# Splitting the output projection of all eight output blocks into two halves of the contraction

## The chip, the cores and the metric

The kernel runs on one core of one Trainium2 chip. The metric is the device time of one execution in microseconds (us). Before the change it is 1344.11 us, the median of three runs (1343.78 to 1345.62).

## The reference

The reference is one step of a hybrid decoder trunk with two layers, in fp32, on 512 prompt tokens and 8 sequences of 4 tokens (544 columns in all), with a model width of 1024. Cut to what matters here, each layer computes

```
h    = RMSNorm(x) * (1 + scale1) + shift1
proj = h @ w_in                          # q, k, v | u | xr, yg
o    = concat(RMSNorm(attention), RMSNorm(state-space mixer), RMSNorm(recurrent mixer)) @ w_o
x    = x + gate1 * o
h2   = RMSNorm(x) * (1 + scale2) + shift2
x    = x + gate2 * (gelu(conv(h2 @ w_up)) * conv(...)) @ w_down
```

The contraction of `@ w_o` runs over 1024 mixer features: 512 of the attention, 256 of the state-space mixer (S5), 256 of the recurrent one (RG-LRU).

## The kernel before

Everything is kept transposed: features lie on the 128 partitions and tokens on the free axis. The 544 columns are cut into two halves, half 0 with 256 columns and half 1 with 288 (the last 32 are the short sequences). Every product of the large matrices is split for accuracy into three fp32r matmuls (`mm3`, L428): a high part of the weight with a high and a low part of the activation, and a low part of the weight with the high one.

The class `Weights` streams the weights in the order of `weights_order` (L1657). There are six slots (`NW`), each with a high and a low tile; a load is a DMA on SP's queue into one of three staging tiles, a cast on ScalarE to the high part (L416) and a subtraction on VectorE for the low part (L417). A slot is given back by `done`, which at once starts the next load. So the order of the list WO (L43) and the moment of each `done` set when a later weight can be used.

`proj` (L1590 and after) is the output projection. It has eight units i (blocks of 128 output features) and two halves, and the contraction runs over eight chunks k in the order KO = 6, 7, 4, 5, 0, 1, 2, 3: first the recurrent mixer (6, 7), then the state-space mixer (4, 5), last the attention (0 to 3). The chunks 6, 7, 4, 5 are called the first part here, the chunks 0 to 3 the second part. Before the change:

- Three pieces (units 0 to 2, half 0) run their first part and stay open in three PSUM banks (L1617 to L1620).
- Units 0 to 3 run the first part of their other pieces, five pieces in all. `some` (L1606) makes one piece: it waits until its chunks have been emitted, takes a bank, runs the matmuls, and `end` adds gate times the result into x (`residual`, L940) and frees the bank.
- The three open pieces get their second part and end.
- Then come the remaining pieces in a skewed order: (3,0), (4,0), (0,1), (5,0), (1,1), (6,0), (2,1), (7,0), (3,1), then the emission of the normalisation of half 0 for the feed-forward part (`norm_all(0)`), then (4,1), (5,1), (6,1), (7,1). Units 0 to 3 run only their second part here, units 4 to 7 all eight chunks.

After each piece of `some` one `tick` emits the next step of the mixers, with one unit of the attention (its scores, its transposes, its product with v). The last piece of every unit also accumulates the squares of x for the next normalisation (`sq_accum`). The normalisation of half 1 is emitted inside the first group of the feed-forward part (`group`, L911), which runs three units of half 0 first.

The written order is a priority and not the issue order: a list scheduler at compile time places each instruction where its engine is free in its own model, earlier lines first. `urgent` moves the residual and the squares 50 places ahead. On the chip each engine then works in its fixed order. PSUM has eight banks here: `wide` (two pairs) and four single ones, called mb0s in layer 0 and mb1s in layer 1 (fb0, fb1 in the feed-forward part). A bank is chosen when a piece is emitted, the least recently used free one.

Of the kernel before, what the change touches and what calls it, by code (L numbers as in the profile page):

```python
# [39 lines left out]
SKEW = 4  # L40
LAG = 3
KO = (6, 7, 4, 5, 0, 1, 2, 3)
WO = ((4, 8, range(4)), (0, 4, range(4)), (0, 8, range(4, 8)))  # L43
NATT = 1
PIN = True
S12 = (2, 12, 5, 14)
# [210 lines left out]
class Banks:  # L257
# [40 lines left out]
    def one(self, w=512, wide=False, only=None):  # L298

        for z in (only, ()):  # L300
            e = [e for e in self.free if (any(y in e[0] for y in z) if z else not self.apart or self.wide(e[0]) == wide)]
            if e:
                break
        n, b = min(e, key=lambda e: self.used[e[0]])
        self.free.remove((n, b))
        self.touch(n)
        return self.tile[n][:, b, :w]
# [10 lines left out]
def trunk(ctx: ExitStack, tc: tile.TileContext, A, O):  # L318
# [46 lines left out]
    def urgent():  # L365
        return tc.high_priority(HPR)
# [61 lines left out]
    def mm3(out, w, k, r, sl, first, last):  # L428
        a, b = sl
        for i, (wi, ri) in enumerate(((0, 0), (0, 1), (1, 0))):  # L430
            T_.matmul(out, w[wi][:, k, :], r[ri][:, a:b], start=first and i == 0, stop=last and i == 2)  # L431
# [431 lines left out]
    def sq_accum(c, hf):  # L863
        a, b = HALF[hf]
        if c == 0:
            SQ[hf] = sp.tile([128, 288], F32, tag=f"sqacc{hf}", name="sqacc", bufs=1)[:, :b - a]
            act(SQ[hf], x[:, c, a:b], AF.Square)
        else:
            s = W(b - a)
            act(s, x[:, c, a:b], AF.Square)  # L870
            V.tensor_add(SQ[hf], SQ[hf], s)
# [34 lines left out]
    def norm_all(hf, al, sh):  # L906
        yield from norm_stats(hf)
        for _ in norm_half(hf, al, sh, True):
            pass

    def run(g):  # L911
        for _ in g:
            pass
# [26 lines left out]
    def residual(ps, g, c, hf):  # L940
        a, b = HALF[hf]
        stt(x[:, c, a:a + 256], ps[:, :256], g[:, c, 0:1], x[:, c, a:a + 256], OP.mult, OP.add)
        if hf:
            t = sp.tile([128, 32], F32, tag="rs", name="rs")
            tv = t.rearrange("p (b t) -> p b t", t=4)
            V.tensor_tensor(tv, ps[:, 256:288].rearrange("p (b t) -> p b t", t=4),
                            g[:, c, 1:9, None].to_broadcast([128, 8, 4]), op=OP.mult)
            V.tensor_add(x[:, c, NP:NT], x[:, c, NP:NT], t)
# [520 lines left out]
    def background(n=1, lanes=(bg, bga)):  # L1469
        for _ in range(n):  # L1470
            for lane in lanes:
                while lane:
                    try:
                        next(lane[0])
                        break
                    except StopIteration:
                        lane.pop(0)

    def flush():
        while bg or bga:  # L1480
            background()
# [18 lines left out]
    def mixers(l, M):  # L1500
# [66 lines left out]
        for n, i in enumerate(WIN_ORDER[l][GRP:]):  # L1567
# [6 lines left out]
            if n == 11 - GRP:  # L1574
                M.win_done = True
                PS.apart = not UNAP
            start(i, p)
        proj(l, M, tick)

    def proj(l, M, tick):  # L1580
        d = LY[l]
        while d["ada"] < 2:
            background()
        g1 = d["mod"][:, 16:24]
        sh2 = d["mod"][:, 24:32]
        def need(k, hf):
            for _ in range(200):
                if (k, hf) in M.o:
                    return
                tick(NTK)  # L1590
            raise RuntimeError(("never ready", k, hf, M.left))

        def part(o, i, hf, k, first, last):
            a = 0 if i > 3 or k < 4 else 4
            mm3(o, W_[("wo", l, a, i)], k - a, hs[k], HALF[hf], first, last)

        def end(i, hf, o, last=True):
            with urgent():
                residual(o, g1, i, hf)
                PS.put(o)  # L1600
                if last:
                    sq_accum(i, hf)
            if hf:
                W_.done(("wo", l, 0 if last else 4, i))

        def some(i, hf, ks, last=True):  # L1606
            for k in ks:
                need(k, hf)
            o = one(HALF[hf][1] - HALF[hf][0], True, PLAST[0] if (i, hf) in PLAST[1] else ())
            for k in ks:  # L1610
                part(o, i, hf, k, k == ks[0], k == ks[-1])
            end(i, hf, o, last)
            tick()

        o = [one(256, True) for i in range(GRP)]
        for k in KO[:4]:
            need(k, 0)  # L1617
            for i in range(GRP):
                part(o[i], i, 0, k, k == KO[0], False)
        for i in range(4):  # L1620
            for hf in range(2):
                if (i, hf) not in ((0, 0), (1, 0), (2, 0)):
                    some(i, hf, KO[:4], False)
        for k in KO[4:]:
            need(k, 0)
            for i in range(GRP):
                part(o[i], i, 0, k, False, k == KO[-1])
        for i in range(GRP):
            end(i, 0, o[i])
        for i, hf in skewed(GRP):  # L1630
            some(i, hf, KO if i > 3 else KO[4:])
            if (i, hf) == (7 - SKEW, 1):
                flush()
                run(norm_all(0, d["al2"], sh2))
        late.append(norm_all(1, d["al2"], sh2))
        assert not M.CH.c
        PS.apart = False

    def skewed(skip=0):
        seq = []  # L1640
        for i in range(8 + SKEW):
            if skip <= i < 8:
                seq.append((i, 0))
            if i >= SKEW:
                seq.append((i - SKEW, 1))
        return seq
# [11 lines left out]
    def weights_order():  # L1658
        for l in range(L):
            for i in WIN_ORDER[l]:  # L1660
                yield ("win", l, i), A["win"][l, i], 8
            for a, b, u in WO:
                for i in u:
# [218 lines left out]
```

## Time and profile before

| | |
|---|---|
| median of three runs | 1344.11 us |
| time of the profiled execution | 1342.55 us |
| span, first to last instruction | 1340.8 us |
| TensorE matmul busy | 1275.7 us (95%) |
| VectorE busy | 871.8 us (65%) |
| ScalarE busy | 599.7 us (45%) |
| mean granted TensorE clock | 0.982 of full |

Busy time of TensorE is the union of modelled matmul durations, so a stretch at half the clock also counts as busy; the column of the granted clock has to be read beside it. PE is TensorE, DVE is VectorE, ACT is ScalarE, SP is the queue that issues most DMAs. Times in the rows are counted from the start of the span. In the output projections nearly all matmuls have the one line L431, in the helper `mm3`; the output tile (mb0s, mb1s, wide) and the width (256 or 288) tell the pieces apart.

### The profile page before, as it was taken

The page shows a single profiled execution, that of the slowest core. Times are in us where ns is not written, and L with a number is a line of the kernel's source. Part 1 is how long each engine was busy: PE and PEld are TensorE (multiplying, and loading weights), DVE is VectorE, ACT ScalarE, POOL GpSimd, SP SyncE. Part 2 cuts the span into 40 slices and gives each one's busy share as a digit, 9 for nine tenths or more (in the row PEclk, how much of TensorE's full clock was granted, in tenths as well). Part 3 has the DMA queues.
Part 4 walks back from the last instruction along what each step waited for, and adds up shares of the span by engine and source line. Part 5 has one row for each costly group of instructions (what it writes and reads, how often), then busy time and mean ns, then how long its engine had stood idle before and what let it go on. Part 6 is the DMA issues. An engine that isn't in the chain of part 4 may idle for free.

```text
span 1340.8 us, 26252 instructions
## 1 busy us (share of the span) xinstructions
PE 1275.7 (95%) x10406; PEld 1173.5 (88%) x10406; DVE 871.8 (65%) x2521; ACT 599.7 (45%) x1196; POOL 48.7 (4%) x82
## 2 busy tenths in 40 slices
PE   5889988989999999999999999899999999999998
PEld 2666776989989998999999887579999999999998
DVE  7877786987564454545548796668865455645651
ACT  4558756465341333233335558655634234323430
POOL 0121010000110000000000001000000000000000
PEclk8999988999999999999999999898999999999999
DMA  9776660436553454335524533112322322233221
GB/s 355 238 239 212 190 188 15 171 124 208 191 199 112 156 189 160 125 125 189 177 73 139 148 94 87 45 54 79 111 89 70 107 84 85 88 95 95 80 77 51
DMA packets 71099, 178.23 MB, mean 133 GB/s; under 512 B 15376, under 2 KB 22448, under 8 KB 70976
## 3 DMA queue, kind: packets, MB, share of 16 engines
q1 hardware_dynamic: 64096, 162.08, 37.7%
q0 software_dynamic: 4960, 11.68, 2.7%
q10 hardware_dynamic: 1920, 2.79, 0.8%
q8 instruction: 82, 1.34, 0.4%
q14 instruction: 41, 0.34, 0.1%
HBM read 159.37 MB, written 14.34 MB: 130 GB/s over the span
## 4 chain that ended last, share of the span: by engine, by line
PE 63%; DVE 4%; ACT 3%; DMA 2%; issue 1%; POOL 0%; SPq 0%; DVEq 0%; POOLq 0%; ACTq 0%
PE wide L431 33%; PE fb1w L431 9%; PE fb0w L431 7%; PE fb1s L431 4%; PE mb1s L431 3%; PE fb0s L431 3%; PE fb0s L577 2%; DMA araw<-in_wada_dram 1%; ACT pm L378 1%; PE mb1s L1282 1%; DVE f L381 1%; DMA f<-kscr 0%; ACT whi L416 0%; ACT L378 0%; PE mb1s L1121 0%
## 5 line engine op out<-in xcount | busy, mean ns | idle before, releaser
L431 PE MATMUL wide<-hh,whi 128*128 128x256 f32 (+1 forms) x1368 | 402.0, 295 | 5.0 <-ACT hh L937 2.0
L431 PE MATMUL wide<-hl,whi 128*128 128x256 f32 (+1 forms) x1368 | 399.6, 292 | 0.0
L431 PE MATMUL wide<-hh,wlo 128*128 128x256 f32 (+1 forms) x1368 | 396.9, 290 | 0.0
L417 DVE TENSOR_TENSOR wlo<-raw,whi 128x1024 fp32r<-128x1024 f32 (+2 forms) x184 | 212.1, 1153 | 195.8 <-ACT whi L416 191.9
L416 ACT CAST whi<-raw 128x1024 fp32r<-128x1024 f32 (+2 forms) x184 | 182.4, 991 | 317.6 <-PE wide L431 171.9
L431 PEld LDWEIGHTS wide<-hh,whi 128*128 128x128 f32 x1368 | 258.9, 190 | 21.1 <-issue 11.2
L431 PEld LDWEIGHTS wide<-hh,wlo 128*128 128x128 f32 x1368 | 261.2, 191 | 2.5 <-issue 2.3
L431 PEld LDWEIGHTS wide<-hl,whi 128*128 128x128 f32 x1368 | 259.7, 190 | 4.0 <-issue 3.6
L431 PE MATMUL wide<-mid,whi 128*128 128x256 f32 (+1 forms) x582 | 111.3, 288 | 0.0
L381 DVE SCALAR_TENSOR_TENSOR f<-wide,prm,f 128x511 f32<-128x511 f32 x236 | 100.0, 484 | 0.0
L431 PEld LDWEIGHTS wide<-mid,whi 128*128 128x128 f32 x582 | 91.4, 188 | 0.4 <-issue 0.4
L937 ACT CAST mid<-f 128x544 fp32r<-128x544 f32 x44 | 28.5, 647 | 127.5 <-DVE f L1718 124.2
L431 PE MATMUL wide<-mid,wlo 128*128 128x256 f32 (+1 forms) x291 | 83.8, 288 | 0.0
L378 ACT ACTIVATE f<-f 128x544 f32<-128x544 f32 x50 | 33.0, 659 | 87.4 <-DVE f L1708 82.5
L431 PE MATMUL fb1w<-hh,whi 128*128 128x256 f32 (+1 forms) x240 | 69.3, 289 | 2.0 <-ACT hh L903 1.5
L431 PE MATMUL fb1w<-hl,whi 128*128 128x256 f32 (+1 forms) x240 | 69.5, 290 | 0.0
L431 PE MATMUL fb1w<-hh,wlo 128*128 128x256 f32 (+1 forms) x240 | 68.9, 287 | 0.0
L431 PE MATMUL fb0w<-hh,whi 128*128 128x256 f32 (+1 forms) x224 | 66.0, 295 | 2.4 <-ACT hh L903 2.4
L381 DVE SCALAR_TENSOR_TENSOR x<-wide,mod,x 128x256 f32<-128x256 f32 x53 | 25.6, 483 | 63.4 <-PE wide L431 63.3
L431 PE MATMUL fb0w<-hl,whi 128*128 128x256 f32 (+1 forms) x224 | 65.0, 290 | 0.0
L431 PE MATMUL fb0w<-hh,wlo 128*128 128x256 f32 (+1 forms) x224 | 64.7, 289 | 0.0
L378 ACT ACTIVATE pm<-pm,st 128x256 f32<-128x256 f32 (+3 forms) x128 | 57.4, 476 | 11.3 <-DVE st L1284 9.2
(612 smaller groups left out, 2558.2 us busy)
## 6 DMA issues: line engine op xcount, KB each, us to landing
raw<-in_wup_dram SPq DMA_DIRECT2D x88, 512.0 KB, 3.6
araw<-in_wada_dram SPq DMA_DIRECT2D x28, 1024.0 KB, 5.2
raw<-in_wada_dram SPq DMA_DIRECT2D x29, 512.0 KB, 5.3
raw<-in_wdn_dram SPq DMA_DIRECT2D x32, 448.0 KB, 3.4
raw<-in_win_dram SPq DMA_DIRECT2D x24, 512.0 KB, 4.5
raw<-in_wdn_dram SPq DMA_DIRECT2D x16, 512.0 KB, 3.6
raw<-in_wo_dram SPq DMA_DIRECT2D x16, 256.0 KB, 4.0
raw<-in_wo_dram SPq DMA_DIRECT2D x8, 512.0 KB, 3.7
```

The lines of the kernel that those rows point to most:

```text
L378: return S.activation(out, in_, f, bias=bias, scale=scale, **kw)
L381: return V.scalar_tensor_tensor(out, a, s, b, op0=op0, op1=op1, **kw)
L416: S.copy(hi, raw)
L417: V.tensor_sub(lo, raw, f32(hi))
L431: T_.matmul(out, w[wi][:, k, :], r[ri][:, a:b], start=first and i == 0, stop=last and i == 2)
L577: T_.matmul(ps[32 * g:32 * g + 32], silu[:, k + i, :], raw[:, i, g], start=k + i == 0, stop=k + i == 7, skip_group_check=True)
L937: S.copy(dst[0], src)
L1282: T_.matmul(pv, M.q[c][:, j * 128:j * 128 + 128], M.kz[:, :, k0:k0 + nk], start=True, stop=True)
```

## The change

The number of split units becomes a constant, WOS = 8. All eight units run their first part ahead of the second: three open pieces as before, then thirteen pieces of the first part in place of five, then the second part of all sixteen. The weights come as sixteen half loads for each layer (first parts of units 0 to 7, then second parts) in place of eight half and four whole ones.

```diff
-WO = ((4, 8, range(4)), (0, 4, range(4)), (0, 8, range(4, 8)))
+WOS = 8
+WO = ((4, 8, range(WOS)), (0, 4, range(WOS)), (0, 8, range(WOS, 8)))
...
         def part(o, i, hf, k, first, last):
-            a = 0 if i > 3 or k < 4 else 4
+            a = 0 if i >= WOS or k < 4 else 4
...
-        for i in range(4):
+        for i in range(WOS):
             for hf in range(2):
                 if (i, hf) not in ((0, 0), (1, 0), (2, 0)):
                     some(i, hf, KO[:4], False)
...
         for i, hf in skewed(GRP):
-            some(i, hf, KO if i > 3 else KO[4:])
+            some(i, hf, KO if i >= WOS else KO[4:])
             if (i, hf) == (7 - SKEW, 1):
                 flush()
                 run(norm_all(0, d["al2"], sh2))
```

## Rows read from the trace of the kernel before

**Rows 1.** Windows, layer 1: length, PE, PEld, DVE, ACT, POOL busy, clock, DMA, GB/s.
```profile
858.20:887.20 29.00, 27.75 (x188) 21.61 (x188) 18.76 (x68) 16.84 (x55) 0.00 (x0) 0.88 0.23 68
887.20:904.08 16.88, 16.88 (x139) 15.56 (x138) 10.44 (x34) 9.45 (x27) 0.00 (x0) 1.00 0.10 32
904.08:907.41 3.33, 0.71 (x5) 0.27 (x3) 3.19 (x14) 0.90 (x3) 0.00 (x0) 0.96 0.00 0
907.41:914.04 6.63, 6.47 (x25) 6.12 (x26) 4.87 (x14) 2.66 (x5) 0.00 (x0) 0.51 0.00 0
...
921.13:936.18 15.05, 15.05 (x114) 14.79 (x113) 14.15 (x42) 9.09 (x16) 0.00 (x0) 1.00 0.35 106
936.18:947.33 11.15, 9.59 (x80) 9.11 (x78) 9.91 (x34) 4.14 (x9) 0.00 (x0) 1.00 0.46 141
```
**Rows 2.** Waits of PE from 840 to 960: us in total, times, longest.
```profile
PE mb1s L431 <- ACT hh L937: 2.1, 2, 1.1
...
PE wide L479 <- DVE qr L381: 1.6, 1, 1.6
PE fb1w L431 <- ACT hh L903: 1.5, 1, 1.5
```
**Rows 3.** ScalarE's timeline in layer 1: start, us; the weight casts of units 6, 7.
```profile
911.46 1.05 ACT L416 CAST whi<-raw 128x1024 fp32r<-128x1024 f32 x1 [2.76 <-PE mb1s L431]
...
914.10 1.05 ACT L416 CAST whi<-raw 128x1024 fp32r<-128x1024 f32 x1 [0.99 <-PE wide L431]
```
**Rows 4.** Windows, layer 0, the same columns as of layer 1.
```profile
226.20:259.60 33.40, 33.34 (x258) 33.13 (x259) 31.31 (x113) 12.42 (x21) 0.00 (x0) 0.95 0.38 127
259.60:274.56 14.96, 14.96 (x115) 14.78 (x113) 14.88 (x44) 7.38 (x12) 1.67 (x3) 1.00 0.59 194
274.56:288.93 14.37, 10.68 (x97) 9.46 (x95) 13.08 (x43) 6.08 (x14) 0.54 (x1) 1.00 0.45 131
288.93:298.00 9.07, 9.07 (x56) 8.97 (x57) 5.95 (x25) 6.60 (x15) 0.00 (x0) 0.81 0.14 56
```
**Rows 5.** Chain that ended last, 921 to 960: start, us: a half-1 piece, four chunks.
```profile
921.29 1.60 PE mb1s L431 x12
```
**Rows 6.** The chain in layer 1, 840 to 960: a half-0 piece of eight chunks.
```profile
918.49 2.81 PE wide L431 x24
```
**Rows 7.** VectorE's timeline: first low parts of the next activations, layers 0 and 1.
```profile
273.07 1.67 DVE L381 SCALAR_TENSOR_TENSOR hl<-half,mod,hh 128x256 fp32r<-128x256 f32 x4
...
929.79 1.27 DVE L381 SCALAR_TENSOR_TENSOR hl<-half,mod,hh 128x256 fp32r<-128x256 f32 x3
```
**Rows 8.** VectorE by line and form, 921.13 to 947.33: busy us, mean ns.
```profile
L417 DVE TENSOR_TENSOR wlo<-raw,whi 128x1024 fp32r<-128x1024 f32 x5 | 6.1, 1218 | 0.0
L381 DVE SCALAR_TENSOR_TENSOR half<-x,al,sqacc 128x256 f32<-128x256 f32 x8 | 3.4, 477 | 0.0
...
L871 DVE TENSOR_TENSOR sqacc<-sqacc,half 128x288 f32<-128x288 f32 x6 | 2.7, 452 | 0.2
L381 DVE SCALAR_TENSOR_TENSOR x<-mb1s,mod,x 128x256 f32<-128x256 f32 x5 | 2.4, 476 | 0.1
...
L948 DVE TENSOR_TENSOR x<-x,rs 128x32 f32<-128x32 f32 x5 | 0.9, 182 | 0.0
L946 DVE TENSOR_TENSOR rs<-mb1s,mod 128x32 f32<-128x32 f32 x5 | 0.9, 179 | 0.0
```
**Rows 9.** VectorE by line and form, 259.60 to 288.93: two of five table groups.
```profile
L612 DVE TENSOR_TENSOR f<-pw,f 128x384 f32<-128x384 f32 x2 | 1.1, 554 | 0.0
...
L616 DVE TENSOR_TENSOR f<-pw,f 128x384 f32<-128x384 f32 x1 | 0.5, 548 | 0.0
```
**Rows 10.** Line L417 over the span: ns min/median/max, forms.
```profile
L417 DVE TENSOR_TENSOR wlo<-raw,whi x184: 678/1224/1228, 21.2 to 1301.6; 128x1024 fp32r<-128x1024 f32 x136, 128x896 fp32r<-128x896 f32 x32, 128x512 fp32r<-128x512 f32 x16
```
**Rows 11.** DMA issues of the page: count, KB each, us to landing.
```profile
raw<-in_wo_dram SPq DMA_DIRECT2D x16, 256.0 KB, 4.0
raw<-in_wo_dram SPq DMA_DIRECT2D x8, 512.0 KB, 3.7
```

## The prediction

> **What bounds the kernel now.** I read the page first: in the table, PE's busy time of 95% of the span says that time can only come from PE's few gaps, from stretches at the lower clock, or from other work that delays PE. The 40 slices of the page put the gaps into the mixers and just behind them, so I cut the two output projections into windows and read the waits, the chain and the engines' timelines there.
>
> Layer 1 is where the change has something to win. PE works on at full clock until 904.08, and then in 3.33 us it is busy for only 0.71; the next 6.63 us run at a granted clock of 0.51, which is the 1.2 GHz level [rows 1]. The waits name the end of the attention's normalisation, 1.6 us for its scale and 2.1 us in all for the casts of its output [rows 2]. Why PE had nothing else is in ScalarE's timeline: the weights of units 6 and 7 are cast at 911.46 and 914.10 only, since a slot comes free when (0,1) and (1,1) are done, and these wait for the attention of half 1 [rows 3].
>
> Layer 0 has no such hole: from 226.20 to 274.56 PE is busy 33.34 of 33.40 and 14.96 of 14.96 us [rows 4]. What a split could fill there is nothing.
>
> Behind both projections stands a second limit. The last piece of half 0, (7,0), ends at about 259.6 and 921.1. From there the normalisation of half 0, the last residuals and squares, and the weights of the next matrix all pass VectorE; the first half-1 matmul of the feed-forward part comes at 288.93 and 947.33. VectorE is busy 14.88 + 13.08 of 29.33 us in the one layer and 14.15 + 9.91 of 26.20 us in the other [rows 1, 4].
>
> **Part 1: what the stall gives back.** In layer 1 the idle time is 3.33 - 0.71 = 2.6 us, and the low clock costs 6.63 x (1 - 0.51) = 3.2 us, together 5.8 us [rows 1]. A half-1 piece of four chunks takes 1.60 us [rows 5]; a half-0 piece of eight takes 2.81, so one of four 1.41 [rows 6]. The change frees the first parts of units 4 to 7 from the attention: 4 x (1.41 + 1.60) = 12.0 us, less any part that ran early anyway. After 887.2 there are then 12.0 us of first parts, 8 x 1.41 = 11.3 us of half-0 second parts and some attention for the 20.2 us up to 907.41. PE no longer runs dry; I take the whole 5.8 us. Nothing hides what is late next: the half-0 pieces behind it. The bounds are 0 (the added pieces wait on banks) and 5.8 plus 1.25, the idle part of the window from 858.20 [rows 1]. In layer 0 the value is 0, bounds 0 and 0.1 [rows 4].
>
> **Part 2: what moves ahead of the normalisation.** Before, the four pieces (4,1) to (7,1) run all eight chunks behind (7,0). After, their first parts, 4 x 1.60 = 6.4 us [rows 5], run ahead of it. PE's total is the same, so (7,0) ends 6.4 us later in each layer, less what part 1 gives: layer 0 at 259.6 + 6.4 = 266.0, layer 1 at 921.1 - 5.8 + 6.4 = 921.7. The cover behind (7,0) shrinks from 15 us [rows 1, 4] to 8.6. The first low part of the new activations is complete 9.1 us behind (7,0) in layer 1 (929.79 plus one third of 1.27) and 13.9 us in layer 0 (273.07 plus a quarter of 1.67) [rows 7]. So PE also idles at the start of the feed-forward part, by 0.5 to 5 us. That idle is no term of its own as long as half 1 comes later still.
>
> **Part 3: the stretch from (7,0) to half 1.** Its VectorE work is not reduced: five low parts of weights at 1.218 us, sixteen instructions of 0.477 of the half-0 normalisation, six residuals, seven sums of squares, two scale calculations [rows 8]. In layer 1 it took 26.20 us with VectorE 24.06 busy; behind 921.7 it ends at 947.9, which is 0.6 us later than now. The bounds are -1.5 (only the busy 24.06) and +2.5 (idle as now, and two residual groups of 0.84 more queued behind). In layer 0 it took 29.33 us, of which nine instructions on tables for the next layer at about 0.55 us make 4.9 us (in five groups of rows, of which the first and the last stand in [rows 9]). They are not needed here. The bounds from 266.0 are 23.1 us (busy time without tables, +0.2) and 29.3 us (all of it again, +6.4). I take 26.2 us, the row of layer 1, which has the same work without tables: 292.2, so +3.3.
>
> **Part 4: the added instructions.** Per layer there are eight more residuals: four of half 0 at 0.476 and four of half 1 at 0.476 + 0.182 + 0.179 = 0.84 us, 5.3 us [rows 8]. Eight half-size low parts at 0.68 in place of four whole ones at 1.22 add 0.6 us [rows 10]. All 5.9 us fall on VectorE ahead of (7,0). In layer 1 it is busy 18.76 + 10.44 of 45.9 us there, which hides them [rows 1]. In layer 0 it is busy 31.31 of 33.40 us [rows 4], but tables and other early work fill its holes, and the stretch grows by 6.4 us. I take 0; if the cover fails, 5.9 - 2.1 = 3.8 us at most in layer 0, and no reason gives a gain. Queued behind an urgent residual on VectorE are the attention's masks, and for these PE's transposes; each can be late by 0.5 us, which costs nothing while PE has pieces. Per layer there are four more load triggers on SP, and the half loads land in 4.0 us against 3.7 [rows 11]; three staging tiles and 3 us of PE for a unit hide that. Eight more ticks per layer find the attention already emitted: 0.
>
> **Part 5: the clock.** PE's idle time ahead of half 1 grows in layer 1 from 1.5 us [rows 2] to some 5: its pieces end near 930.4, three units of half 0 fill 8.4. After the comparable gap in layer 0 the stretch from 288.93 ran at 0.81 and took 9.07 us [rows 4]. Layer 1 fell to no low clock there; I take 0.4 us, from 0 to 9.07 x 0.19 = 1.7.
>
> The Trainium skill has a rule that speaks against the change, in "TensorE: Matmul & The Clock Gate", section "A second HAM failure mode: psum-queue depth-cycling": a kernel that cycles its groups through the banks lets PE idle briefly between groups, and the clock swings. Here the pieces on rotating banks from 921.13 to 936.18 show PE busy 15.05 of 15.05 us at clock 1.00 [rows 1], so no term comes of it; by the rule the last rival below gains weight.
>
> **The sum.** Layer 0 +3.3, layer 1 +0.6 + 0.4: +4.3 us. On the profiled execution of 1342.55 us (span 1340.8 and 1.75 around it) that is 1346.9; this execution lies 1.56 us under the median of 1344.11, so the median is forecast at 1348.4 us.
>
> **The rivals.** All times are on the median.
>
> *Rival 1, not slower: half 1 follows PE and not VectorE.* If the scheduler puts the weights of the fourth to sixth feed-forward unit (3 x 1.22 us) behind the normalisations, half 1 comes 11.15 us after PE's pieces, as now, and 947.33 becomes 941.5; layer 0 keeps its time. 1344.1 - 5.8 = 1338.3. It decides where VectorE's work behind (7,0) falls to 8.6 + 11.15 = 19.8 us; 24.06 less 3.7 is 20.4, just short. For it: PE's stall in layer 1 is real and goes. Against it: VectorE's 92% in this stretch.
>
> *Rival 2, the two effects cancel.* Both stretches shrink to their busy work: +0.2 in layer 0, -1.5 + 0.4 in layer 1, so 1343.2. For it: with less cover the scheduler has fewer holes to fill with tables. Against it: in layer 1 VectorE was left idle for 2.1 of 26.20 us without any table [rows 1].
>
> *Rival 3, banks and tables.* Three banks stay held across thirteen pieces in place of five, and the attention and the pieces share the other five. If bank waits take half of the 5.8 us, and layer 0 keeps its tables (+6.4), the sum is 6.4 + 2.9 + 0.6 + 1.7 = +11.6: 1355.7. Against it: five pieces already share those banks, and from 887.20 PE is busy throughout [rows 1].
>
> **How the numbers follow.** Forecast 0.34, rival 1 0.22, rival 2 0.24, rival 3 0.20. A difference of 0.2%, 2.7 us, is about what a measurement of this kernel tells from no change. Faster by more: rival 1 and 0.02 of rival 2, 0.24. Within it: the other 0.22 of rival 2 and 0.05 of the forecast, whose bounds begin below +2.7: 0.27. Slower by more: the other 0.29 of the forecast and rival 3, 0.49. Both signs hold much, so the range goes from 1337.0, a little below rival 1, to 1357.0, a little above rival 3; the forecast's own range is 1342.8 (+0.2, -1.5) to 1353.0 (+6.4, +2.5).
>
> **What would show it.** Right: in layer 1 no stretch near a clock of 0.5 between 900 and 920 and no idle there; (7,0) at about 921 in layer 1 and 266 in layer 0; then VectorE above 90% until the half-1 matmuls, with PE idle for several us ahead of them, in both layers. Wrong: half-1 matmuls of the feed-forward part in layer 1 well before 945, or PE waiting on residuals between the added pieces, or the projection of layer 0 ending earlier than now.

## The result and the profile after

The change makes the kernel slower: 1352.54 us median (1350.88 to 1353.18, 4 runs) against 1343.94 of the kernel before in the same runs (1343.40 to 1345.62), a ratio of 1.0069, 95% interval 1.0050 to 1.0088. That is +8.6 us where +4.3 was forecast; 1352.54 lies inside the range. The profiled execution after took 1350.88 us (span 1349.1), against 1342.55 (1340.8) before. One execution each of b_skew2_l0 (2820.05 us) and e_h0_notab (4262.69 us) was slow, and their medians below leave it out.

The windows of layer 1 after the change, from the end of the attention to half 1 of the feed-forward part (columns as in [rows 1]):

```profile
887.00:913.00 26.00, 25.33 (x186) 22.16 (x187) 19.81 (x69) 13.71 (x38) 0.00 (x0) 0.95 0.10 31
913.00:925.60 12.60, 12.60 (x105) 12.60 (x104) 11.57 (x34) 6.45 (x13) 0.00 (x0) 1.00 0.46 146
925.60:934.00 8.40, 8.39 (x63) 7.96 (x61) 7.90 (x24) 4.61 (x7) 0.00 (x0) 1.00 0.44 131
934.00:939.88 5.88, 0.53 (x2) 0.19 (x2) 5.54 (x14) 2.14 (x5) 0.00 (x0) 0.81 0.68 207
939.88:951.00 11.12, 11.12 (x76) 11.00 (x76) 8.67 (x27) 4.54 (x11) 0.00 (x0) 0.79 0.20 77
951.00:954.40 3.40, 0.52 (x3) 0.19 (x3) 2.58 (x13) 1.85 (x5) 0.00 (x0) 1.00 0.00 0
954.40:962.30 7.90, 7.90 (x47) 7.90 (x48) 5.83 (x24) 5.59 (x14) 0.00 (x0) 0.78 0.01 3
```

The hole of [rows 1], 3.33 us with PE busy for 0.71 and 6.63 us at 0.51, is gone: from 887 to 934 PE is busy 46.3 of 47.0 us. In its place stands another, behind the last half-1 piece. (7,0) ends at 925.60, the half-1 pieces last until 934.00, then PE is busy for 0.53 of 5.88 us. The half-0 group of the feed-forward part runs at a granted clock of 0.79, and the first 8 us of half 1 at 0.78.

Layer 0, the same columns:

```profile
225.65:264.00 38.35, 38.35 (x308) 38.13 (x309) 37.38 (x136) 13.19 (x25) 1.13 (x2) 1.00 0.39 122
264.00:272.30 8.30, 8.30 (x63) 7.95 (x61) 8.21 (x27) 4.82 (x7) 0.00 (x0) 1.00 0.48 170
272.30:276.67 4.37, 0.44 (x3) 0.19 (x2) 4.32 (x12) 2.19 (x5) 0.00 (x0) 0.86 0.65 201
276.67:288.30 11.63, 11.63 (x76) 11.46 (x76) 9.30 (x24) 4.60 (x11) 0.54 (x1) 0.76 0.37 129
288.30:293.50 5.20, 1.54 (x19) 0.61 (x18) 4.21 (x21) 1.85 (x5) 0.54 (x1) 0.90 0.62 212
```

In [rows 4] PE went from the pieces into the half-0 group without a gap, at clock 1.00. Now it runs dry here too.

PE's waits from 840 to 970 after the change (us in total, times, longest), which answer to [rows 2]:

```profile
PE mb1s L480 <- DVE qr L382: 3.4, 1, 3.4
PE fb1w L432 <- ACT hh L904: 2.4, 1, 2.4
PE fb1w L432 <- ACT hh L379: 1.9, 1, 1.9
```

The first and the third are the new gap: the scale of the half-0 normalisation, and its first cast. In [rows 2] the 1.6 us for a scale and the 2.1 us for the attention's casts stood in the old hole.

VectorE's timeline, layer 0 and layer 1: start, us, and in brackets the idle time ahead of it:

```profile
287.82 0.42 DVE L467 TENSOR_REDUCE cs<-fb0s 128x2 f32<-128x256 f32 x1 [2.33 <-PE fb0s L465]
...
949.05 0.42 DVE L467 TENSOR_REDUCE cs<-fb1s 128x2 f32<-128x256 f32 x1 [2.14 <-PE fb1s L465]
```

This is the start of the half-1 normalisation. VectorE stands idle for over 2 us in both layers until PE has done the transposes of its sums; in PE's order these stand behind most of the half-0 group. So the stretch from (7,0) to half 1 is no longer full of VectorE work: by the windows above VectorE is busy 26.0 of 29.5 us in layer 0 (88%) and 24.7 of 28.8 us in layer 1 (86%), where [rows 1, 4] have 95% and 92%. The prediction had named more than 90% as a sign that it was right.

**One table for all runs.** Two profiles can differ by some us long before the projection, so times are counted from one matmul per layer that all kernels have, the product with tile ks in the attention (the mark below):

```profile
205.78 0.63 PE L1403 MATMUL mb0s<-ks,f 128*128 128x32 f32 x4
...
874.28 0.63 PE L1403 MATMUL wide<-ks,f 128*128 128x32 f32 x4
```

From PE's timeline of each kernel, in us: the end of (7,0); cover, the half-1 pieces behind it up to their end; gap, PE's pause until the half-0 group; tail, from (7,0) to the first half-1 matmul; and that matmul itself. The rows below "after" are the runs of the next section: the change in one layer only; the banks given back early (e_hold); only the half-0 pieces of units 4 to 7 split (e_h0), and the same with two products put off (e_h0_ada); the kernel before with less cover in layer 0 (b_skew2_l0); the change with more cover (e_skew5), with the scale calculation first (e_prio), without the added residuals (e_nores) and with the tables put off (a_notab); the last version (h1_notab); and e_h0 with the tables put off (e_h0_notab).

```
                 layer 0                          layer 1
              (7,0) cover  gap  tail half 1   (7,0) cover  gap  tail half 1
before        52.79 14.94   0  29.30  82.09   51.36 15.06   0  26.20  77.56
after         58.07  8.29 4.53 29.65  87.72   51.22  8.33 6.05 28.90  80.12
layer 0 only  59.17  8.30 4.53 28.78  87.95   49.68 15.05   0  26.19  75.87
layer 1 only  53.17 15.01   0  29.34  82.51   50.17  8.35 5.88 28.32  78.49
e_hold        58.65  8.30 4.53 29.67  88.32   49.82  8.50 5.91 28.62  78.44
e_h0          53.39 14.99   0  32.65  86.04   45.33 14.90   0  28.55  73.88
e_h0_ada      51.94 15.03   0  33.17  85.11   46.36 14.90   0  28.56  74.92
b_skew2_l0    57.71  9.81 3.37 26.77  84.48   48.64 15.07   0  26.21  74.85
e_skew5       60.15  7.55 3.86 28.05  88.20   52.14  8.00 4.23 28.83  80.97
e_prio        59.17  8.30 3.37 28.69  87.86   50.88  8.36 4.53 28.14  79.02
e_nores       58.49  8.36 5.97 28.87  87.36   50.43  8.35 5.92 28.18  78.61
a_notab       59.25  8.35 5.98 29.49  88.74   51.64  8.35 5.93 28.41  80.05
h1_notab      51.36 15.06   0  26.16  77.52   45.38 14.97   0  28.59  73.97
e_h0_notab    52.52 15.37   0  28.41  80.93   45.38 14.96   0  28.59  73.97
```

Where two kernels have the same code in a layer, the table shows what a single profile is worth. Layer 0 unchanged: 82.09 and 82.51. Layer 1 unchanged: 77.56, 75.87 and 74.85, mean 76.1, all of the spread ahead of (7,0); the profile on which the prediction rests was the slowest of the three. Its 1.7 us against layer 0 only do not come from the hole: 12 to 18 us behind the mark, in the attention, its granted clock is 0.72 (881.77 to 887.77), where the other two have 1.00. The hole itself is as large in layer 0 only, and about 1 us smaller in b_skew2_l0. Layer 1 changed: 80.12 and 78.49, mean 79.3.

The loss, then: layer 0, 87.72 - 82.09 = +5.6; layer 1, 79.3 - 76.1 = +3.2; and from half 1 of layer 1 to its first down-projection matmul 90.04 us against 88.79, +1.2, with the clock at 0.78 in the first 8 us. Together +10.0 from single profiles, inside the interval of the times (+6.7 to +11.8).

### The profile page after: what moved, and what is told of

It is laid out like the page before. It is cut to its first block, busy times and chain, and to the rows that moved or that the text cites. A ratio compares the mean times of both kernels' runs of the same rounds, so it can differ in the third digit from the quotient of the medians.

```text
span 1349.1 us, 26341 instructions
## 1 busy us (share of the span) xinstructions
PE 1279.1 (95%) x10406; PEld 1176.7 (87%) x10406; DVE 880.3 (65%) x2561; ACT 601.4 (45%) x1204; POOL 48.8 (4%) x82
## 4 chain that ended last, share of the span: by engine, by line
PE 63%; DVE 5%; ACT 3%; DMA 2%; issue 1%; POOL 0%; SPq 0%; DVEq 0%; POOLq 0%; ACTq 0%
PE wide L432 34%; PE fb1w L432 9%; PE fb0w L432 6%; PE fb1s L432 4%; PE fb0s L432 3%; PE mb1s L432 2%; PE fb0s L578 1%; PE mb1s L1283 1%; DMA araw<-in_wada_dram 1%; ACT pm L379 1%; DVE f L382 1%; ACT whi L417 1%; DVE wlo L418 1%; DMA f<-kscr 0%; ACT L379 0%
## 5 line engine op out<-in xcount | busy, mean ns | idle before, releaser
L432 PE MATMUL wide<-hh,whi 128*128 128x288 f32 (+1 forms) x1384 | 407.7, 296 | 3.9 <-ACT e L1015 1.6
L432 PE MATMUL wide<-hl,whi 128*128 128x288 f32 (+1 forms) x1384 | 404.9, 293 | 0.0
L432 PE MATMUL wide<-hh,wlo 128*128 128x288 f32 (+1 forms) x1384 | 402.6, 291 | 0.0
L417 ACT CAST whi<-raw 128x1024 fp32r<-128x1024 f32 (+2 forms) x192 | 184.0, 958 | 331.4 <-PE wide L432 171.7
L432 PEld LDWEIGHTS wide<-hh,whi 128*128 128x128 f32 x1384 | 263.0, 191 | 20.7 <-issue 11.2
L432 PEld LDWEIGHTS wide<-hl,whi 128*128 128x128 f32 x1384 | 263.5, 190 | 4.0 <-issue 3.5
L432 PEld LDWEIGHTS wide<-hh,wlo 128*128 128x128 f32 x1384 | 264.9, 191 | 2.4 <-issue 2.1
L382 DVE SCALAR_TENSOR_TENSOR x<-wide,mod,x 128x256 f32<-128x256 f32 x60 | 28.9, 482 | 61.4 <-PE wide L432 60.8
```

The costliest lines, as they stand in the source:

```text
L382: return V.scalar_tensor_tensor(out, a, s, b, op0=op0, op1=op1, **kw)
L417: S.copy(hi, raw)
```

## The experiments

I call the first theory *cover*: the half-1 first parts of units 4 to 7, 6.4 us of PE work, now run ahead of the half-0 normalisation instead of behind (7,0); PE runs dry, loses the clock, and half 1 comes later. Its rivals are the held banks, VectorE's added work, and the tables of the next layer.

**Each layer alone.** The number of split units becomes a table by layer, (8, 4) for layer 0 only and (4, 8) for layer 1 only:

```diff
-WOS = 8
+WOSL = (8, 4)
...
+        WOS = WOSL[l]
```

> All eight units split in layer 0 only; layer 1 keeps four split and four whole units. Cover theory (the half-1 first parts of units 4 to 7, 6.4 us of PE work, go ahead of the half-0 normalisation, and PE runs dry behind (7,0)): layer 0 pays as in the full change, +4.6 us up to the first half-1 matmul of the feed-forward part and up to 1 us behind it, so about +5.2 us, 1349; layer 1 keeps its idle hole and its stretch near 0.5 of the clock after 904. Rival (the held banks cost where the attention waits for banks, that is in layer 1): layer 0 alone is within 1.5 us of before, 1344 to 1345.5.

> All eight units split in layer 1 only. Cover theory: layer 1 wins its hole (5 to 6 us) and gives it back behind (7,0): +1.4 us up to half 1 and +1.2 us at the lower clock behind it, about +2.6 us, 1346.5; the two single-layer results add up to the whole, +8.6, within 2 us. Rival (the loss of layer 1 in the full change came from layer 0, by a shifted schedule): layer 1 alone is faster than before by the hole, 1338 to 1341, and the sum of the two runs misses +8.6 by over 4 us.

Measured: layer 0 alone 1348.27, ratio 1.0043 (1.0024 to 1.0062), +5.8 us; layer 1 alone 1346.21, 1.0027 (1.0011 to 1.0043), +3.6 us. They add up to +9.4 against +8.6: both layers pay, independently. Layer 0 has no hole to fill, and by the table it pays the more; the intervals of the two times overlap.

**The banks given back early.** The first parts of units 4 to 7 go behind the end of the three held pieces, and the order of the weight loads (WO, not shown) follows:

```diff
-        for i in range(WOS):
+        for i in range(4):
             for hf in range(2):
                 if (i, hf) not in ((0, 0), (1, 0), (2, 0)):
                     some(i, hf, KO[:4], False)
...
+        for i in range(4, 8):
+            for hf in range(2):
+                some(i, hf, KO[:4], False)
```

> The split of all eight units as in the change, but the three held pieces are finished and their banks given back where before.py gave them back, behind the first parts of units 0 to 3; the first parts of units 4 to 7 follow, still ahead of the normalisation. Bank theory (three banks held across thirteen pieces instead of five are what costs): at least half of the +8.6 us comes back, 1344 to 1348. Cover theory: the same 6.4 us stand ahead of the normalisation, so as the change within 2 us, 1350.5 to 1354.5; in layer 1 a hole may come back in part, since the held pieces wait for the attention before the added parts may run.

Measured: 1353.18, 1.0084 (1.0062 to 1.0106), and the row of the table is that of the change. The bank theory falls.

**Only the half-0 pieces of units 4 to 7 split.**

```diff
-WO = ((4, 8, range(WOS)), (0, 4, range(WOS)), (0, 8, range(WOS, 8)))
+WO = ((4, 8, range(8)), (0, 4, range(4)), (0, 8, range(4, 8)))
...
-            for hf in range(2):
+            for hf in range(2 if i < 4 else 1):
...
-            some(i, hf, KO if i >= WOS else KO[4:])
+            some(i, hf, KO if i > 3 and hf else KO[4:])
```

> Only the half-0 pieces of units 4 to 7 are split; their half-1 pieces run all eight chunks behind the half-0 normalisation, as in before.py (the upper half of these four weights is loaded twice). Cover theory: PE's cover behind (7,0) is 15 us again, so layer 0 comes to its half-1 matmuls as before (+0 to +1 us), and layer 1 has 4 x 1.41 = 5.6 us of added first parts for its hole and keeps 3 to 5.8 us of gain: 1338.5 to 1342. Bank theory (three banks held across nine pieces): between before and the change, 1347 or more. VectorE theory (the added residuals and low parts are the price; four of eight residuals and all the extra low parts remain): 1347 to 1350.

Measured: 1347.24, 1.0028 (1.0010 to 1.0046), outside what cover expected and inside what its two rivals did. The table splits the miss. Layer 1 does part of what cover says: (7,0) at 45.33, no gap, half 1 at 73.88 against 76.1 and 79.3; but the tail is 28.55 and not 26.2, so 2.2 us are kept and not 3 to 5.8. In layer 0 the gap is gone, and yet half 1 comes at 86.04. PE's timeline there (the last bracket is the idle time and its releaser):

```profile
291.41 0.43 PE L480 MATMUL fb0s<-eye,qr 128*128 128x128 f32 x2 [2.64 <-DVE qr L382]
294.38 1.91 PE L578 MATMUL fb0s<-araw,cin 128*32 128x256 f32 x10 [2.54 <-DMA araw<-in_wada_dram]
```

The scheduler has put a second modulation product ahead of half 1, and it waits for its transfer. The next run, e_h0 with one more edit, puts those products off:

```diff
-            background()
+            background(1, (bg,))
+            n = 2 * f + v
+            background(1 if l or n > 5 else 2 * (n > 2), (bga,))
```

> The kernel with only the half-0 pieces of units 4 to 7 split, and in layer 0 the two modulation products that stood ahead of half 1 of the feed-forward part put off by three units (there one of them waited 2.54 us for its transfer, and half 1 came 3.5 us later, while layer 1 gained 3.7 us). Cover theory: layer 0 is as before within 1 us and layer 1 keeps its 3.7 us: 2.5 to 4.5 us faster than before, -0.2 to -0.35%. Bank or VectorE theory: the transfer only hid another loss, so layer 0 stays 2 to 4 us late and the time is 0 to +0.3% of before.

Measured: 1344.36, 1.0018 (1.0003 to 1.0034). Half 1 of layer 0 is still at 85.11, so the transfer had hidden another loss, as the rival said. In the profiles it is VectorE. In layer 0 of e_h0, from (7,0) to half 1:

```profile
263.58:278.57 14.99, 14.98 (x114) 14.74 (x113) 14.98 (x47) 8.21 (x15) 0.00 (x0) 1.00 0.51 166
278.57:296.23 17.66, 12.48 (x106) 10.03 (x105) 17.56 (x60) 7.18 (x16) 1.67 (x3) 0.92 0.51 164
```

VectorE is busy 32.54 of 32.65 us, and in e_h0_ada 33.06 of 33.17, where [rows 4] have 27.96 of 29.33. In both kernels 19 table instructions of 8.1 us stand in this stretch, against nine of 4.9 us before. Why they moved there was not tried; the upper weight halves, loaded twice, may have pushed them behind. That the tables cost here is shown by e_h0_notab below.

**The cover cut with no split added.** before.py with another distance in layer 0:

```diff
+PSK = (2, 4)
...
-        for i, hf in skewed(GRP):
+        for i, hf in skewed(GRP, PSK[l]):
...
-            if (i, hf) == (7 - SKEW, 1):
+            if (i, hf) == (7 - PSK[l], 1):
```

> before.py, with no added split; only in layer 0 the half-1 pieces of the output projection follow the half-0 pieces at a distance of two units instead of four, so that (3,1) and (4,1), 1.60 + 3.2 = 4.8 us, move ahead of (7,0) and of the half-0 normalisation. Cover theory: (7,0) ends 4.8 us later, PE runs dry behind (7,1), and half 1 of the feed-forward part of layer 0 starts 4 to 5 us later: +4 to +6.5 us in all, 0.3 to 0.5%. Rivals (the held banks, or the eight added residuals and the extra low parts on VectorE): nothing of these is here, so within 1.5 us of before.

Measured: 1341.79, 0.9997 (0.9985 to 1.0009): no change, and cover as I had it falls short. Its windows of layer 0, from (7,0) on:

```profile
263.07:272.88 9.81, 9.81 (x76) 9.74 (x74) 9.78 (x29) 3.17 (x5) 1.67 (x3) 1.00 0.55 187
272.88:276.25 3.37, 0.60 (x5) 0.20 (x3) 3.27 (x9) 1.98 (x4) 0.54 (x1) 1.00 0.66 233
276.25:289.84 13.59, 12.38 (x94) 11.19 (x94) 10.52 (x38) 5.58 (x14) 0.00 (x0) 0.87 0.14 40
```

(7,0) ends 4.9 us later and PE pauses for 3.4 us, as expected; but the tail shrinks from 29.30 to 26.77, and half 1 comes only 2.4 us later. VectorE is busy 23.6 us in the tail in place of 28.0 [rows 4]: two groups of residuals and squares went ahead with their pieces, and two low parts of weights. So part of the price of a late (7,0) seems to be given back when VectorE's work goes ahead with the piece; no run separates this. In the change nothing goes ahead: the five half-1 residuals with their squares still stand behind (7,0).

**More cover in the change.** The same edit in the changed kernel, with a distance of five in both layers:

```diff
+PSK = (5, 5)
```

> The change as it is, with a distance of five units in place of four in both layers: (3,1) moves from ahead of the half-0 normalisation to behind it, so the cover grows by 1.60 us per layer. Cover theory: (7,0) and with it half 1 come 1.6 us earlier in each layer, and PE idles 1.6 us less: 3 to 4.5 us faster than the change, +0.3 to +0.45% of before instead of +0.65%. Bank or VectorE theory: the same pieces, banks and instructions, so the time of the change within 1.5 us.

Measured: 1353.56, 1.0089 (1.0069 to 1.0109). It tells nothing of cover: the scheduler mixed (7,0) with the half-1 pieces, and the work behind it is 7.55 us in place of 8.29, not 9.9.

**The scale calculation first.**

```diff
-                run(norm_all(0, d["al2"], sh2))
+                with urgent():
+                    run(norm_all(0, d["al2"], sh2))
```

> The change as it is, with the half-0 normalisation given the high priority that the residuals have, so that VectorE runs its scale calculation ahead of low parts of the feed-forward weights (two of 1.22 us less between the sums and the scale). Cover theory: PE's cover is short by the length of this chain, so a chain 2 to 3 us shorter takes as much of PE's idle time ahead of half 0 (5.9 us in layer 1) away; half 1 gains less, since the low parts only move behind: 1 to 4 us faster than the change in all. If VectorE's total work in this stretch alone set the end (the forecast's step), the idle moves and half 1 starts where it did: the time of the change within 1 us.

Measured: 1353.11, 1.0086 (1.0068 to 1.0105). The gap is 1.2 and 1.5 us shorter and the tail 1.0 and 0.8 us, 1.8 us in all. The time is within the 1 us of the change that the rival named, and cover's 1 to 4 us faster do not show; but the two ratios come from two sets of runs, each with an interval of some 0.2% to either side, so this settles little.

**VectorE's added work, taken away in two ways.** The first leaves out the eight added residuals of each layer (so the first parts of units 4 to 7 are missing from the output); the second puts the tables off, behind the last low part of the half-1 normalisation (LAST):

```diff
-                residual(o, g1, i, hf)
+                if last or i < 4:
+                    residual(o, g1, i, hf)
```

```diff
     def tables(l):
-        ssm_params(l)
+        with tc.issue_after(LAST[0].ins):
+            ssm_params(l)
+            lru_params(l)
         yield
-        lru_params(l)
         yield
```

> The change with the same pieces, banks, loads and order, but the eight added residuals per layer (the first parts of units 4 to 7) are left out, so these partial sums are computed and not added. VectorE-sum theory (layer 0 is bound by VectorE from the projection to half 1 of the feed-forward part, 96 us of instructions in 88 against 91 in 82 before, and the added residuals of 5.3 us are the price there): layer 0 comes back by 4 to 5.5 us and layer 1 by 0 to 2.5, so -0.05% to +0.3% of before. Cover theory (PE's pieces stand ahead of the normalisation, whatever VectorE does): the time of the change, +0.55% or more.

> The change as it is, but the tables for the next layer (in layer 0) are put behind the last low part of the half-1 normalisation on VectorE; 9.2 us of them stood between the last mixer steps and half 1 in the change, and 9.2 in before. VectorE-sum theory: layer 0 loses at least its +5.6 us again, 4 to 7 us faster than the change, and layer 1 keeps its +2.5 to +3: +0.1% to +0.35% of before. Cover theory: (7,0) still ends 38 us behind the first chunk, PE still runs dry by 4 us and half 1 follows 28 us later: within 2 us of the change, +0.5% or more.

Measured: 1351.20, 1.0062 (1.0039 to 1.0084), and 1351.03, 1.0060 (1.0038 to 1.0081): both as the change. (The 9.2 us of tables in the expectation are only the products; with the sums between them 48 instructions of 13.7 us stand between the mark and half 1 of layer 0, in the change and before.) Layer 0 of a_notab from (7,0) on:

```profile
267.58:275.93 8.35, 8.35 (x64) 8.09 (x62) 7.99 (x24) 4.65 (x7) 0.00 (x0) 1.00 0.40 126
275.93:281.91 5.98, 0.59 (x4) 0.19 (x3) 5.55 (x14) 2.21 (x5) 0.00 (x0) 0.92 0.73 206
281.91:297.07 15.16, 13.74 (x95) 12.36 (x95) 11.24 (x39) 6.40 (x16) 0.00 (x0) 0.80 0.19 62
```

With no table in the whole stretch the tail is still 29.49 us, and PE waits longer, not less. Neither the residuals nor the tables alone are the price of the change.

**The decisive pair.** e_h0 with the tables put off, to be set against a_notab: the half-1 first parts go back behind the normalisation. Against e_h0:

```diff
-        ssm_params(l)
+        with tc.issue_after(LAST[0].ins):
+            ssm_params(l)
+            lru_params(l)
```

> In both layers only the half-0 pieces of units 4 to 7 are split (their half-1 pieces stay whole and behind the half-0 normalisation), and the tables are behind the half-1 normalisation as in a_notab. Against a_notab, which reached half 1 of layer 0 some 88.7 us behind the last mixer mark, this takes the half-1 first parts (6.4 us of PE work) from ahead of the normalisation to behind it. Cover theory: (7,0) at 52 to 53.5 us instead of 59.3 and half 1 at 80 to 82 in layer 0; layer 1 at 74 to 75 against 80; with the low clock avoided 12 to 16 us under a_notab, -0.35% to -0.6% of before. Theory that any added split costs (four more residuals, four upper weight halves loaded and reduced twice): layer 0 at 85 or later, -0.2% to +0.2%.

Measured: 1341.00, 0.9987 (0.9971 to 1.0003). In layer 0, from (7,0) on:

```profile
262.88:278.25 15.37, 15.22 (x115) 14.77 (x114) 14.46 (x41) 8.10 (x15) 0.00 (x0) 1.00 0.53 162
278.25:291.29 13.04, 11.16 (x97) 9.57 (x95) 11.28 (x38) 5.28 (x12) 0.00 (x0) 1.00 0.31 88
291.29:299.29 8.00, 8.00 (x48) 8.00 (x49) 7.45 (x39) 5.60 (x14) 0.00 (x0) 0.79 0.30 121
```

No gap and clock 1.00 up to half 1, which comes at 80.93 and 73.97 against 88.74 and 80.05: -7.8 and -6.1 us, in the bounds of cover (in layer 1 at their edge). The low clock was not avoided: the first 8 us of half 1 run at 0.79 in both layers. The times of the two differ by 0.73% of before, some 10 us, where cover expected 12 to 16. Against before no gain is clear, and 0.9987 lies among the times of the rival, which had layer 0 at 85 or later. The pair differs in four residuals per layer too (e_nores: no price) and in the upper halves loaded twice, which works against e_h0_notab. Set against e_h0, which has its tables in the stretch, half 1 of layer 0 comes 5.1 us earlier (86.04 to 80.93), and 4.2 us earlier than in e_h0_ada: this is the price of the tables there.

What the pair shows is narrower than the name cover. Of the -7.8 and -6.1 us, (7,0) itself has -6.7 and -6.3; the tail goes from 29.49 to 28.41 in layer 0 and from 28.41 to 28.59 in layer 1, though PE no longer pauses. So the price shown is that 6.4 us of pieces stand ahead of (7,0), and half 1 follows (7,0) by 28.4 to 29.5 us in either order. That PE's pause itself costs is not shown by it: in layer 1 of e_h0_notab VectorE is busy 27.2 of the 28.6 us of the tail, more work than the 24.1 us before, and this alone may keep it as long.

**A version that beats both.** Layer 0 as in before.py with the tables put off; layer 1 with only the half-0 pieces of units 4 to 7 split. Beside the edit of the tables:

```diff
-WO = ((4, 8, range(WOS)), (0, 4, range(WOS)), (0, 8, range(WOS, 8)))
+WO = [((4, 8, range(n)), (0, 4, range(4)), (0, 8, range(4, 8))) for n in (4, 8)]
...
-            for hf in range(2):
+            for hf in range(2 if i < 4 else 1):
```

> Aimed at beating both: layer 0 as in before.py, with the tables put behind the half-1 normalisation as in a_notab; layer 1 with the half-0 pieces alone of units 4 to 7 split. VectorE-sum theory: layer 0 reaches half 1 some 2 to 3.5 us earlier than before (PE waited 3.7 us there), layer 1 is 1 to 2.5 us earlier, so -3 to -6 us, -0.2 to -0.45%. Cover theory: layer 0 was bound by PE's order, so only layer 1's part: -1 to -2.5 us, -0.1 to -0.2%.

Measured: 1335.48 us, ratio 0.9941 (0.9918 to 0.9963), -0.6%. That is more than either theory gave; the interval still reaches the -0.45% of the VectorE-sum theory and leaves out the cover theory's -0.2%. With 15 us of cover PE kept pace, and there the tables did cost: without them the tail of layer 0 is 26.16 us, that of layer 1, and half 1 comes 4.6 us earlier (1.4 us of this ahead of (7,0)). Half 1 of layer 1 comes 2.1 us earlier (73.97 against the mean of 76.1), but behind it 1.3 us go back (90.12 us to the first down-projection matmul against 88.79), again with the first 8 us at 0.79. So most of the gain is that of the tables; the two edits were not run apart, and the profiled execution was the fastest of its seven (1331.21 us).

## Why the prediction was right, and where its size was off

The forecast had the direction and half of the size, +4.3 us against +8.6. It gave slower by more than 0.2% a chance of 0.49 only, and its range held both signs, so that 1352.54 lies inside says little.

*Part 1, right.* The hole went. In layer 1 (7,0) ended at a mean of 50.7 (after and layer 1 only), against 49.9 in the three unchanged profiles: 0.8 us later, where 6.4 - 5.8 = 0.6 was forecast.

*Part 2, right in its mechanism.* In layer 0 (7,0) came 5.3 us later, in the kernel with layer 0 only 6.4. The cover fell to 8.3 us (8.6 forecast), and PE idled 4.5 and 6.0 us, the second above the forecast's 0.5 to 5. e_h0_notab against a_notab shows that these four pieces are what layer 0 pays for.

*Part 3, the term that was mis-sized, and for a wrong reason.* I took 26.2 us of tail for layer 0, on the argument that tables would give way: 3.3 us. It stayed at 29.65, so layer 0 cost 5.6, near the upper bound of 6.4. That is not because the tables stayed: four of the nine instructions, 2.2 us, were left behind (7,0), and a_notab has none and 29.49. In layer 1 the tail grew from 26.2 to 28.9 and 28.3, where the forecast kept it: the layer cost 3.2 us against the mean of 76.1, where 0.6 was forecast with a bound of +2.5 (the terms given for that bound, 0.6 and twice 0.84, make 2.3). My reason, VectorE as the limit behind (7,0), holds in the kernel before, as h1_notab shows, and not in the changed one. Once PE has run dry, the path as I read it in the trace is a chain through both: two low parts of weights on VectorE ahead of (7,0)'s last sum in layer 1 (4.25 us from (7,0) to the transposes of the sums, against 1.7), the scale, the casts, the half-0 group at 0.76 to 0.79 of the clock, the half-1 sums behind it in PE's order, and only then the half-1 normalisation. The trace shows these steps in this order; moving one of them by itself was tried only in e_prio, and it settled little.

*Part 4, right.* Without the added residuals the time is the same.

*Part 5, too small.* 0.4 us taken, bounded by 1.7; the low clock behind half 1 of layer 1 cost 1.2 us, and the one in the half-0 groups is inside the tails. The pieces on rotating banks ran at clock 1.00 from 264.00 to 272.30 and from 925.60 to 934.00; in the stretch up to half 1 the clock fell only behind PE's wait for the scale. The rule of the Trainium skill that was weighed ("TensorE: Matmul & The Clock Gate", section "A second HAM failure mode: psum-queue depth-cycling") therefore made no term here, as the trace of before had it.

*The rivals.* Half 1 followed neither PE's pieces (rival 1) nor VectorE's bare busy time (rival 2). Of rival 3 the banks are refuted by e_hold; its number for layer 0 came out for another reason.

What stays open: why 5.1 us of cover cut by order alone (b_skew2_l0) cost nothing in the whole, where the 6.7 us of the change cost 5.6 in the same layer. The shorter tail explains 2.5 us of it. Of the other 2.4, 1.3 come back behind half 1 (104.76 us to the first down-projection matmul against 106.07 before), where the first 8 us ran at a clock of 1.00 against 0.79 before. The 1.1 us that are left lie within the interval of the times, 1.6 us to either side. Open too is what keeps the tail of the changed kernel at 28 to 30 us, since neither the tables nor the residuals alone do.

## What to carry to other kernels

Splitting a contraction fills a stall, but the added first parts come out of the work that covered the next serial step; count what is left behind that step's trigger, and where it is less than the chain's length, move only the part that fills the hole (here half 0 of layer 1, not half 1 of both layers). Even that was worth little here, 2.1 us at half 1 and 1.3 of them lost again behind it. Before you cost a tail by one engine's busy time, ask whether that engine stays full when its partner runs dry: here putting off the same 13.7 us of tables was worth 4.6 us with full cover and nothing without. And take a stage's time from more than one profile: layer 1 reached half 1 1.7 and 2.7 us sooner in two other profiles of the same code, and 1.7 us of each was a low clock in the attention and not the hole.

## What was not expected of the hardware

The clock came back late. In the changed kernel a pause of PE of 4.4 to 5.9 us was followed by 11 us at 0.76 to 0.79, between the two levels in the mean, and the second pause, ahead of half 1, by low stretches again: 2.9 us of it (3.40 - 0.52) by 0.78 in layer 1, and 3.7 us (5.20 - 1.54) by this in layer 0:

```profile
293.50:302.40 8.90, 8.89 (x47) 8.90 (x48) 5.84 (x25) 5.42 (x14) 0.00 (x0) 0.67 0.06 24
```

In e_h0_notab, 1.9 us (13.04 - 11.16) in layer 0 were followed by 8 us at 0.79. In b_skew2_l0, where PE paused there for 1.2 us (13.59 - 12.38), the first 8 us of half 1 ran at 1.00:

```profile
289.84:297.84 8.00, 8.00 (x58) 7.83 (x59) 6.18 (x25) 6.84 (x15) 0.00 (x0) 1.00 0.39 133
```

So the longer pauses ahead of half 1 cost more than their length, and this is how a loss in layer 1's projection still grew by 1.2 us behind it.
